# A residual block on one Trainium2 core: buffers of the first weight blocks, place of the forget logits' transposes, a transpose by DMA, and the engine of the last sums

## The chip, the cores and the metric

The kernel runs on one core of a Trainium2 chip. The metric is the device time of one execution in microseconds (us). A core has five instruction streams that run side by side and meet only through semaphores: TensorE (PE, its weight loads are listed as PEld), VectorE (DVE), ScalarE (ACT), GpSimd (POOL), and SyncE (SP), which here only issues DMAs.

## The reference

One layer of a hybrid encoder block; x is 256 tokens x 1024, all in fp32.

```python
h = rmsnorm(x, ffn1_pre_g)
x = x + 0.5 * rmsnorm(swiglu(h, ffn1_w_in, ffn1_w_down), ffn1_post_g)      # 1024 -> 2 x 2816 -> 1024

h = rmsnorm(x, mix_pre_g)
q_a, f_a, i_a, g_a, q_b, k_b, v_b, f_b, gates = split(h @ w_in)             # f_b: 8 forget logits a token
o_a = rmsnorm(hgrn2(q_a, f_a, i_a), hg_norm_g) * silu(g_a)                  # gated linear recurrence, 8 heads
c   = cumsum(log_sigmoid(f_b + fox_f_bias), axis=tokens)                    # 8 x 256
s   = q_b . k_b / sqrt(128) + c[query] - c[key], causal                     # 8 heads
o_b = softmax(s) @ v_b
y   = sigmoid(gate_a) * (o_a @ w_branch_a) + sigmoid(gate_b) * (o_b @ w_branch_b)
x   = x + rmsnorm(y @ w_out, mix_post_g)

x = x + rmsnorm(cross_attention(rmsnorm(x, mem_pre_g), rmsnorm(mem, mem_kv_g)), mem_post_g)
h = rmsnorm(x, ffn2_pre_g)
x = x + 0.5 * rmsnorm(swiglu(h, ffn2_w_in, ffn2_w_down), ffn2_post_g)
```

## The kernel before, in words

**Weights.** All large weights (some 145 MB) are read once, in units of 128 x 1024 floats (512 KB). `load_split` (L120) loads a unit into a buffer of the ring `raw` (four buffers), ScalarE casts it to `hi` (L128), VectorE computes the remainder `lo` (L129), and each product is made of three: hi.hi, hi.lo, lo.hi. The `raw` buffer is free for another load when `lo` is done. `hi` and `lo` have eight buffers each. SyncE issues the loads in program order and waits, in its own queue, for the buffer that the next load needs.

**Head.** The first four units, which are chunk 0 of the first FFN's input weights, come in another form: eight `head` blocks of 128 x 776 floats, block kb holding the kb-th 128 rows of x transposed (256 columns), the same rows of the weights (512) and the gains (8). The eight tiles share the four buffers of `raw` (L462). For each block ScalarE casts the weights (L475) and, but for the first, the x part (L262), and VectorE computes both remainders (L263, L477). Behind the head stand four ordinary units (chunk 1), then x itself in token order (`xs`, two loads, L482), whose place in SyncE's queue is given by `X_AT` (not ahead of the load with that number), and the columns of gains and the bias (L484, L485).

**First FFN.** Its gain is folded into the x part, and the token's 1/rms (`rstd`) is applied when a product is evacuated. Chunks 0 and 1 are computed first (`act_first`, L371: per block of 128 rows six products of 128 x 512, two token halves times three), into four PSUM banks; only then `norm_1` gives rstd from `xs` by ScalarE's sums of squares (L234) and a chain of small VectorE operations (L214 to L230). The evacuations (`act_evac`, L356 and L361) follow, mixed with the splits of the units of chunk 2, which is computed in the same manner.

**Forget logits.** They are the last eight columns of a group of weights with g_a; `zf` (128 x 8, one tile for each half of the tokens, L709) holds them times rstd. `forget(m)` (L717) turns both to 8 x 128 on TensorE, put behind product m of the log of products (`after` makes the scheduler issue them not before that product; they need not stand together), and then makes the bias, log-sigmoid (ScalarE) and running sum (VectorE) into `cc` (8 x 256). POOL stores `cc` to DRAM as `cd` (L733). It is called with m + 30, where m is the number of the first product of k_b's first half.

**Attention scores.** POOL loads `cd` back as rows spread to all partitions: `cbc` (L781) and two `cbm` (L785), on which it puts the causal mask (L788). The same sums as columns, `ct` (128 x 16), come from two transposes of `cc` on TensorE and a copy by VectorE (L794, L795). `fox_scores` (L799) uses them: VectorE adds `ct` and subtracts `cbc` or `cbm` (L817, L819), ScalarE makes the exponentials (L822).

**Gates.** Four bias rows `brow` (L878) have two buffers, which the early keys `E` of the recurrence (L582) use before them.

**End.** `post_last` (L302) computes the last half of the tokens: squares, rstd, then `x + t * r`. Columns 0 to 511 and 768 to 1023 are done by VectorE and stored through SyncE's queue, columns 512 to 767 by ScalarE (scaling), POOL (sum) and a store from ScalarE's queue (L325 to L333). For the first half of the tokens, and for the other layers, `post` does it in two VectorE operations of 512 columns (L298).

Of the kernel before, what the change touches and what calls it, by code (L numbers as in the profile page):

```python
# [11 lines left out]
F32 = mybir.dt.float32  # L12
F32R = mybir.dt.float32r
I32 = mybir.dt.int32
AF = mybir.ActivationFunctionType
ALU = mybir.AluOpType
AX = mybir.AxisListType

P = 128
D = 1024  # L20
T = 256
KB = D // P
# [25 lines left out]

WARM = 8

X_AT = 10


_ORDER = [
# [15 lines left out]
def block_kernel(ctx: ExitStack, tc: tile.TileContext, wts, head_in, gf_in, x_in, mem_in, memT_in, cols, rows, fbias, masks, out):  # L70
    nc = tc.nc
    V, S, G, PE = nc.vector, nc.scalar, nc.gpsimd, nc.tensor

    cp = ctx.enter_context(tc.tile_pool(name="consts", bufs=1))
    wp = ctx.enter_context(tc.tile_pool(name="weights", bufs=4))
    mp = ctx.enter_context(tc.tile_pool(name="data", bufs=21))
    sp = ctx.enter_context(tc.tile_pool(name="small", bufs=8))
# [5 lines left out]
    def MM(*args, **kw):  # L83
        log.append(PE.matmul(*args, **kw).ins)  # L84
# [9 lines left out]
    def nm(s):  # L94
        count[0] += 1
        return f"{s}_{count[0]}"

    def m4(shape, dt=F32, n="m"):
        return mp.tile(shape, dt, tag="m4", name=nm(n))

    def s1(n=1, dt=F32, name="s"):
        return sp.tile([P, n], dt, tag=f"s{n}", name=nm(name), bufs=16)
# [7 lines left out]
    def trp():  # L110
        return pp.tile([P, 512], F32, tag="tr", name=nm("tr"), bufs=2)
# [5 lines left out]
    def parts_of():  # L117
        return [wp.tile([P, D], F32R, tag=t, name=nm(t), bufs=8) for t in ("hi", "lo")]
# [31 lines left out]
    class Pair:  # L150


        def __init__(self, n=2):
            self.h, self.l = [], []
            for _ in range(n):
                self.more()
# [39 lines left out]
    ones = cp.tile([P, P], F32, name="ones")  # L196
    V.memset(ones, 1.0)
    ident = cp.tile([P, P], F32, name="ident")
    make_identity(nc, ident)

    warm = s1(name="warm")
# [31 lines left out]
    def ssq(dst, src):  # L233
        S.activation(junk[:, : src.shape[-1]], src, AF.Square, accum_out=dst)  # L234
# [67 lines left out]
    def post_last(ps, h, grow, factor):  # L302

        s = s1(2, name="ss2")
        ts = []
        for j in range(2):
            ssq(s[:, j : j + 1], ps[j])
            if j == 0:
                sums = s1(name="v")
                V.tensor_scalar(out=sums, in0=s[:, 0:1], scalar1=D * EPS, scalar2=None, op0=ALU.add)  # L310
            else:
                y = s1(name="y")
                S.activation(y, s[:, 1:2], AF.Sqrt, bias=sums)
                v = s1(name="v")
                V.tensor_tensor(out=v, in0=s[:, 1:2], in1=sums, op=ALU.add)
            t = sp.tile([P, 512], F32, tag="z2", name=nm("post"), bufs=3)
            V.scalar_tensor_tensor(out=t, in0=ps[j], scalar=-factor * 16.0, in1=grow[:, j * 512 : (j + 1) * 512], op0=ALU.mult, op1=ALU.mult)
            ts.append(t)
        z = s1(name="y")
        V.reciprocal(z, y)  # L320
        t = s1(name="t")
        V.scalar_tensor_tensor(out=t, in0=v, scalar=z, in1=z, op0=ALU.mult, op1=ALU.mult)
        r = s1(name="y")
        V.scalar_tensor_tensor(out=r, in0=t, scalar=3.0, in1=z, op0=ALU.subtract, op1=ALU.mult)
        for eng, a, b, queue in ((G, 512, 768, nc.scalar), (V, 0, 512, nc.sync), (V, 768, 1024, nc.sync)):  # L325
            xh = xs[:, h, a:b]
            t = ts[a // 512][:, a % 512 : a % 512 + b - a]
            if eng is G:
                S.activation(t, t, AF.Copy, scale=r)
                G.tensor_tensor(out=xh, in0=t, in1=xh, op=ALU.add)  # L330
            else:
                V.scalar_tensor_tensor(out=xh, in0=t, scalar=r, in1=xh, op0=ALU.mult, op1=ALU.add)
            queue.dma_start(out[h * P : (h + 1) * P, a:b], xh)  # L333


    def ffn(w_in, w_dn, X, r2, n_tok, i_row, first_half, second_half=None):
# [122 lines left out]


    X1 = Pair()
    heads = [wp.tile([P, D], F32, tag="raw", name=nm("head"), bufs=4) for _ in range(KB)]  # L462
    for kb in range(KB):
        loads.append(nc.sync.dma_start(heads[kb][:, : T + 512 + KB], head_in[kb]).ins)

    S.activation(warm, ones[:, 0:1], AF.Silu)
    wps = trp()
    for _ in range(WARM):
        MM(wps[:, :P], ones, ones, start=True, stop=True)
    for kb in range(KB):  # L470
        if kb % 2 == 0:
            cache[_AT["f1_in"] + kb // 2] = parts_of()
        hi, lo = (p[:, kb % 2 * 512 : kb % 2 * 512 + 512] for p in cache[_AT["f1_in"] + kb // 2])
        w = heads[kb][:, T : T + 512]
        S.copy(hi, w)  # L475
        gain_split(X1, kb, heads[kb][:, :T], heads[kb][:, T + 512 + kb : T + 512 + kb + 1], first=kb == 0)
        V.tensor_tensor(out=lo, in0=w, in1=hi.bitcast(F32), op=ALU.subtract)  # L477

    def norm_1():
        with tc.issue_after(loads[X_AT]):  # L480
            for h in range(2):
# [20 lines left out]
    for h in range(2):  # L502
        m = len(log)
# [70 lines left out]
    class Rec:  # L574


        def __init__(self, g):
            self.g, self.f = g, fT[g]
            self.aux = m4([P, D], n="aux")

            self.ATd = self.aux[:, 256:512]
            self.E = sp.tile([P, 512], F32, tag="brow", name=nm("early"), bufs=2)  # L582
            self.T = [self.aux[:, 512:], sp.tile([P, T], F32, tag="tq", name=nm("tq"), bufs=2)]
            G.memset(self.ATd, 0.0)
            self.AT = self.f
            self.cur = self.f.rearrange("p b h t -> p (b h t)")
            self.li = 0
# [126 lines left out]
    cc = sp.tile([8, T], F32, tag="fz", name="cc", bufs=1)  # L714
    cd = dp.tile([8, T], F32, name="cd")

    def forget(m):  # L717
        pf = trp()
        with after(m):
            for h in range(2):  # L720
                PE.transpose(pf[0:8, h * P : (h + 1) * P], zf[h], ident)
        V.tensor_scalar(out=fz, in0=pf[0:8, :T], scalar1=fb_s, scalar2=None, op0=ALU.add)
        V.scalar_tensor_tensor(out=fa, in0=fz, scalar=-1.0, in1=fz, op0=ALU.mult, op1=ALU.max)
        with tc.issue_after(sig_last):
            S.activation(fa, fa, AF.Exp, scale=-1.0)
        S.activation(fa, fa, AF.Ln, bias=1.0)
        V.scalar_tensor_tensor(out=fa, in0=fz, scalar=0.0, in1=fa, op0=ALU.min, op1=ALU.subtract)
        for h in range(2):
            cv, fv = (t[:, h * P : (h + 1) * P] for t in (cc, fa))
            if h:  # L730
                cv, fv = cv[:, ::-1], fv[:, ::-1]
            V.tensor_tensor_scan(out=cv, data0=ones[0:8, 0:1].to_broadcast([8, P]), data1=fv, initial=cc[:, P - 1 : P] if h else 0.0, op0=ALU.mult, op1=ALU.add)
        G.dma_start(cd, cc)  # L733
# [3 lines left out]
    for c in range(2):  # L737
        for name, lst, sc in (("k_b", kb_, 1.0), ("q_b", qb_, 1.0 / math.sqrt(128.0))):
            u = chunk(name, c)
            t = m4([P, 4, T], n=name)  # L740
            m = len(log)
            for j in range(2):
                ps = proj_col2(X2, u, (2 * j, 2 * j + 1))
                for i in range(2):
                    V.scalar_tensor_tensor(out=t[:, 2 * j + i], in0=ps[:, i], scalar=sc, in1=row2, op0=ALU.mult, op1=ALU.mult)
            lst.append(t)
            if c == 0 and name == "k_b":
                forget(m + 30)


    for li, m in enumerate(LEVELS + (64, 128)):
# [14 lines left out]
    for h in range(2):  # L766
# [8 lines left out]
        r = rstd_x(ps)  # L775
        for j in range(2):
            V.scalar_tensor_tensor(out=Gt[h][:, j * 512 : (j + 1) * 512], in0=ps[j], scalar=r, in1=Gt[h][:, j * 512 : (j + 1) * 512], op0=ALU.mult, op1=ALU.mult)


    cbc = m4([P, 8, P], n="cbc")  # L780
    G.dma_start(cbc, cd[:, 0:P].partition_broadcast(P))  # L781
    cbm = []
    for g in range(2):
        t = m4([P, 4, T], n="cbm")
# [2 lines left out]
            tv = t[:, :, b * P : (b + 1) * P]  # L787
            G.affine_select(out=tv, in_=tv, pattern=[[0, 4], [-sign, P]], compare_op=ALU.is_ge, fill=BIG, base=0, channel_multiplier=sign)  # L788
        cbm.append(t)

    ct = s1(16, name="ct")
    pc = trp()
    for h in range(2):
        PE.transpose(pc[:, h * 8 : h * 8 + 8], cc[:, h * P : (h + 1) * P], ident[0:8, 0:8])  # L794
    V.tensor_copy(ct, pc[:, :16])  # L795

    ps_, pT0s, pT1s = {}, [], []

# [61 lines left out]
    for c in range(2):  # L860
        u = chunk("v_b", c)
        t = m4([P, 2, 512], n="v_b")
# [12 lines left out]
    def gates(c):  # L875
        u = chunk("gates", c)
        z = m4([P, 2, 512], n="zg")
        brow = sp.tile([P, 512], F32, tag="brow", name=nm("brow"), bufs=2)  # L878
        with tc.issue_after(loads[-1]):
            nc.sync.dma_start(brow, rows[4 + c // 2, c % 2 * 512 : c % 2 * 512 + 512].partition_broadcast(P))  # L880
        for h in range(2):
            ps = mm()
            proj_tok(ps, X2, u, h)
            V.scalar_tensor_tensor(out=z[:, h], in0=ps, scalar=r2[h], in1=brow, op0=ALU.mult, op1=ALU.add)
        zs.append(z)

    m = len(log)
# [20 lines left out]
    for c in range(1, 4):  # L908
        gates(c)
# [14 lines left out]
    for c in range(2):  # L924
        for name, X, zc in (("br_a", OA, c), ("br_b", OB, 2 + c)):
            u = chunk(name, c)
            for h in range(2):
                z = zs[zc][:, h]
                m = len(log)
# [23 lines left out]
    m = len(log)  # L953
# [7 lines left out]
    m = len(log)  # L961
# [5 lines left out]
    m = len(log)  # L967
    for c in range(2):
        u = chunk("mk", c)
        KM.more()  # L970
        for j in range(2):
            js = slice(2 * j, 2 * j + 2)
            ps = proj_col2(M, u, (2 * j, 2 * j + 1))
            t = sp.tile([P, 2, T], F32, tag="z2", name=nm("km"), bufs=3)
# [25 lines left out]
    for h in range(2):  # L1000
        a, b = h * P, (h + 1) * P
# [3 lines left out]
        for i in range(4):  # L1005
            for j in range(2):
                kb = 2 * i + j
# [7 lines left out]
        p = m4([P, 4, T], n="pm")  # L1015
# [27 lines left out]
    m = len(log)  # L1043
# [15 lines left out]
    m = len(log)  # L1059
# [100 lines left out]
```

## Time and profile before

| | |
|---|---|
| median of 3 runs | 797.56 us (797.14 to 797.66) |
| the profiled execution, its own time | 798.41 us |
| its span in the trace | 796.6 us, granted TensorE clock 0.999 |
| ScalarE busy | 426.6 us (54%), x650 |
| VectorE busy | 519.8 us (65%), x824 |
| POOL busy | 11.7 us (1%), x29 |
| read from HBM | 145.67 MB, 184 GB/s over the span |
| head loads | 8, 388 KB each, median 3.8 us to landing |
| weight loads | 248, 512 KB each, median 4.4 us to landing |

Each row of a timeline gives the start, the duration, the engine, the line of the kernel, the operation with output and input, their size, and how many equal ones were merged; in brackets stands how long the engine had been idle and who ended that. An engine name with a q (SPq) is the engine's queue of issues. Rows of groups give minimum, median and maximum duration in ns, and the first and last start. Rows of stretches give the busy time and count on PE, PEld, DVE, ACT and POOL, then the granted clock, the busy share of the 16 DMA engines and GB/s. The rest of an execution's own time, 1.8 us here, lies outside the span.

### The profile page before, as it was taken

The numbers are of one execution on the slowest core, as the hardware profiler recorded it, in microseconds if no ns is written. First come the engines' busy times: TensorE is split into PE (matmuls) and PEld (weight loads), VectorE is DVE, ScalarE is ACT, GpSimd is POOL, SyncE is SP. The second block draws the span as 40 slices with busy tenths as digits, with TensorE's granted clock in tenths as the row PEclk, the third lists the DMA queues.
The fourth block names the chain that finished last, engine by engine and source line by source line (L and its number), as shares of the span: only waits on it lengthen the run. The fifth ranks groups of instructions, "written<-read, shape, count | busy, mean of one in ns | idle before, by whom it ended". The sixth has DMA issues, their size and how long they took to land.

```text
span 796.6 us, 12213 instructions
## 1 busy us (share of the span) xinstructions
PE 787.1 (99%) x4748; PEld 679.3 (85%) x4748; DVE 519.8 (65%) x824; ACT 426.6 (54%) x650; POOL 11.7 (1%) x29
## 2 busy tenths in 40 slices
PE   9999999999999999999999999999999999999996
PEld 7788888887899999998888888999888888888885
DVE  5774544557756997688675665965649754545543
ACT  5774434546754567458574345655647644434541
POOL 0000000000000100300000000000000000000000
PEclk9999999999999999999999999999999999999999
DMA  8886655565455454844486655456443656654521
GB/s 268 289 269 210 227 206 163 172 203 179 161 184 143 128 184 159 290 148 147 151 271 238 207 171 169 157 186 202 149 135 132 215 190 225 198 200 161 186 80 53
DMA packets 43689, 147.52 MB, mean 185 GB/s; under 512 B 4840, under 2 KB 8176, under 8 KB 43632
## 3 DMA queue, kind: packets, MB, share of 16 engines
q1 hardware_dynamic: 43024, 145.03, 54.9%
q0 software_dynamic: 464, 1.58, 0.6%
q8 instruction: 37, 0.61, 0.3%
q14 instruction: 20, 0.16, 0.1%
q10 hardware_dynamic: 144, 0.13, 0.0%
HBM read 145.67 MB, written 1.06 MB: 184 GB/s over the span
## 4 chain that ended last, share of the span: by engine, by line
PE 94%; DMA 3%; DVE 2%; ACT 1%; issue 0%; SPq 0%; DVEq 0%; ACTq 0%
PE mm L84 66%; PE acc L84 24%; PE tr L351 1%; DMA head<-in_head_dram 1%; PE tr L84 1%; DMA xs<-in_x_dram 1%; PE tr L271 1%; DMA raw<-in_wts_dram 1%; PE tr L834 0%; PE tr L920 0%; PE tr L1023 0%; ACT junk L234 0%; DVE lo L477 0%; DVE lT L263 0%; ACT hi L475 0%
## 5 line engine op out<-in xcount | busy, mean ns | idle before, releaser
L129 DVE TENSOR_TENSOR lo<-raw,hi 128x1024 fp32r<-128x1024 f32 (+1 forms) x260 | 311.4, 1206 | 127.7 <-ACT hi L128 118.8
L128 ACT CAST hi<-raw 128x1024 fp32r<-128x1024 f32 (+1 forms) x260 | 267.3, 1038 | 155.7 <-PE mm L84 81.9
L84 PE MATMUL mm<-lo,hT 128*128 128x512 f32 (+1 forms) x592 | 227.2, 386 | 0.7 <-DVE lo L129 0.7
L84 PE MATMUL mm<-hi,hT 128*128 128x512 f32 (+1 forms) x592 | 227.1, 386 | 0.1
L84 PE MATMUL mm<-hi,lT 128*128 128x512 f32 (+1 forms) x592 | 226.1, 385 | 0.0
L84 PEld LDWEIGHTS mm<-hi,hT 128*128 128x128 f32 x592 | 111.1, 188 | 22.4 <-ACT hT L262 0.6
L84 PEld LDWEIGHTS mm<-hi,lT 128*128 128x128 f32 x592 | 111.1, 188 | 21.7 <-DVE lT L263 0.5
L84 PEld LDWEIGHTS mm<-lo,hT 128*128 128x128 f32 x592 | 111.0, 188 | 21.5 <-DVE lo L129 1.1
L84 PE MATMUL acc<-hi,act 128*128 128x512 f32 x352 | 111.9, 390 | 0.0
L84 PE MATMUL mm<-hT,hi 128*128 128x256 f32 x384 | 109.1, 284 | 0.0
L84 PE MATMUL mm<-hT,lo 128*128 128x256 f32 x384 | 109.0, 284 | 0.0
L84 PE MATMUL mm<-lT,hi 128*128 128x256 f32 x384 | 108.9, 284 | 0.0
L84 PEld LDWEIGHTS acc<-hi,act 128*128 128x128 f32 x352 | 66.1, 188 | 13.1
L84 PEld LDWEIGHTS mm<-hT,hi 128*128 128x128 f32 x384 | 73.6, 192 | 0.4 <-PE mm L84 0.3
L84 PEld LDWEIGHTS mm<-hT,lo 128*128 128x128 f32 x384 | 73.6, 192 | 0.1
L84 PEld LDWEIGHTS mm<-lT,hi 128*128 128x128 f32 x384 | 73.6, 192 | 0.1
L84 PE MATMUL acc<-lo,act 128*128 128x512 f32 x176 | 70.0, 398 | 0.0
L356 ACT ACTIVATE sg<-mm,rstd 128x256 f32<-128x256 f32 x40 | 19.0, 475 | 74.8 <-PE mm L84 74.8
L361 DVE SCALAR_TENSOR_TENSOR at<-mm,rstd,sg 128x256 f32<-128x256 f32 x40 | 19.2, 480 | 56.6 <-ACT sg L356 56.6
L84 PEld LDWEIGHTS acc<-lo,act 128*128 128x128 f32 x176 | 33.1, 188 | 6.2
L84 PE MATMUL acc<-hi,hT 128*128 128x512 f32 x96 | 35.8, 401 | 0.1
L84 PE MATMUL acc<-hi,lT 128*128 128x512 f32 x96 | 35.2, 394 | 0.0
(195 smaller groups left out, 648.4 us busy)
## 6 DMA issues: line engine op xcount, KB each, us to landing
raw<-in_wts_dram SPq DMA_DIRECT2D x248, 512.0 KB, 4.4
raw<-in_gf_dram SPq DMA_DIRECT2D x12, 344.0 KB, 3.8
head<-in_head_dram SPq DMA_DIRECT2D x8, 388.0 KB, 3.8
grow<-in_rows_dram SPq DMA_DIRECT2D x4, 512.0 KB, 6.0
xs<-in_x_dram SPq DMA_DIRECT2D x2, 512.0 KB, 7.7
cbm<-cd POOLq DMA_DIRECT2D x2, 512.0 KB, 8.6
brow<-in_rows_dram SPq DMA_DIRECT2D x4, 256.0 KB, 5.0
memT<-in_memT_dram SPq DMA_DIRECT2D x2, 512.0 KB, 6.2
```

The source lines that it names most:

```text
L84: log.append(PE.matmul(*args, **kw).ins)
L128: S.copy(h, r)
L129: V.tensor_tensor(out=l, in0=r, in1=h.bitcast(F32), op=ALU.subtract)
L271: PE.transpose(ps[:, j * P : (j + 1) * P], src(kb), ident)
L351: PE.transpose(trv[:, j, h * P : (h + 1) * P], ats[c, h][:, j * P : (j + 1) * P], ident)
L356: silu = S.activation(sg, ps[:, :FC], AF.Silu, scale=r2[h])
L361: V.scalar_tensor_tensor(out=a, in0=ps[:, FC:], scalar=r2[h], in1=sg, op0=ALU.mult, op1=ALU.mult)
```

## The change

- The eight head blocks get eight buffers: four of `raw`, four of a new ring `extra`. The ring `brow` is gone; the early keys `E` and the four `brow` rows take buffers of `extra` (four) in its place. To make room, the scratch of POOL's DMA descriptors is set to 4096 bytes.
- `X_AT` goes from 10 to 11. In the head, the cast of a block is put behind the VectorE remainder of the block before.
- `forget` is called with m + 46 in place of m + 30.
- `ct` is loaded by two DMAs from `cd`, issued by POOL ahead of `cbc`, in place of two transposes and a copy.
- `post_last` does the last sums in two VectorE operations of 512 columns, both stored through SyncE's queue.

```diff
-X_AT = 10
+X_AT = 11
...
-        for eng, a, b, queue in ((G, 512, 768, nc.scalar), (V, 0, 512, nc.sync), (V, 768, 1024, nc.sync)):
+        for a, b in ((0, 512), (512, 1024)):
             xh = xs[:, h, a:b]
-            t = ts[a // 512][:, a % 512 : a % 512 + b - a]
-            if eng is G:
-                S.activation(t, t, AF.Copy, scale=r)
-                G.tensor_tensor(out=xh, in0=t, in1=xh, op=ALU.add)
-            else:
-                V.scalar_tensor_tensor(out=xh, in0=t, scalar=r, in1=xh, op0=ALU.mult, op1=ALU.add)
-            queue.dma_start(out[h * P : (h + 1) * P, a:b], xh)
+            V.scalar_tensor_tensor(out=xh, in0=ts[a // 512], scalar=r, in1=xh, op0=ALU.mult, op1=ALU.add)
+            nc.sync.dma_start(out[h * P : (h + 1) * P, a:b], xh)
...
-    heads = [wp.tile([P, D], F32, tag="raw", name=nm("head"), bufs=4) for _ in range(KB)]
+    heads = [wp.tile([P, D], F32, tag="raw" if kb < 4 else "extra", name=nm("head"), bufs=4) for kb in range(KB)]
...
-    S.activation(warm, ones[:, 0:1], AF.Silu)
+    warm_last = S.activation(warm, ones[:, 0:1], AF.Silu).ins
...
+    lo_last = warm_last
     for kb in range(KB):
...
-        S.copy(hi, w)
+        with tc.issue_after(lo_last):
+            S.copy(hi, w)
...
-        V.tensor_tensor(out=lo, in0=w, in1=hi.bitcast(F32), op=ALU.subtract)
+        lo_last = V.tensor_tensor(out=lo, in0=w, in1=hi.bitcast(F32), op=ALU.subtract).ins
...
-            self.E = sp.tile([P, 512], F32, tag="brow", name=nm("early"), bufs=2)
+            self.E = wp.tile([P, D], F32, tag="extra", name=nm("early"), bufs=4)[:, :512]
...
-                forget(m + 30)
+                forget(m + 46)
...
+    ct = s1(16, name="ct")
+    for h in range(2):
+        G.dma_start(ct[:, 8 * h : 8 * h + 8], cd[:, h * P : (h + 1) * P].rearrange("e p -> p e"))
     cbc = m4([P, 8, P], n="cbc")
...
-    ct = s1(16, name="ct")
-    pc = trp()
-    for h in range(2):
-        PE.transpose(pc[:, h * 8 : h * 8 + 8], cc[:, h * P : (h + 1) * P], ident[0:8, 0:8])
-    V.tensor_copy(ct, pc[:, :16])
...
-        brow = sp.tile([P, 512], F32, tag="brow", name=nm("brow"), bufs=2)
+        brow = wp.tile([P, D], F32, tag="extra", name=nm("brow"), bufs=4)[:, :512]
...
-    nc = _bacc.Bacc("TRN2", target_bir_lowering=False, num_devices=1)
+    nc = _bacc.Bacc("TRN2", target_bir_lowering=False, num_devices=1, dynamic_dma_scratch_size=4096)
```

## The prediction

> **What bounds the kernel now.** I read the profile's page first, then the list of waits for TensorE, then the timeline of the first 31 us, of the stretch around the forget logits, of the attention scores and of the end.
>
> ```profile
> span 796.6 us, 12213 instructions
> PE 787.1 (99%) x4748; PEld 679.3 (85%) x4748; DVE 519.8 (65%) x824; ACT 426.6 (54%) x650; POOL 11.7 (1%) x29
> ```
> ```profile
> PE mm L84 <- DVE lo L129: 0.7, 1, 0.7
> PE tr L721 <- DVE zf L709: 0.5, 1, 0.5
> ```
>
> TensorE is busy 99% of the span, and once it works it is kept waiting in few places: the first 31 us, one wait on zf, and the tail behind the last product. Everything else runs under the products. So an edit is worth what it takes out of TensorE's stream, out of those stalls, or out of the tail; the other engines count only where they keep TensorE waiting.
>
> **The head.** Three views of it follow (start, duration, engine, line, operation; in brackets the idle time before and who ended it): SyncE's queue, TensorE's weight loads, ScalarE.
>
> ```profile
> 0.75 9.32 SPq L464 DMA_DIRECT2D head<-in_head_dram  x8
> 11.00 5.03 SPq L127 DMA_DIRECT2D raw<-in_wts_dram  x4
> 16.09 0.90 SPq L482 DMA_DIRECT2D xs<-in_x_dram  x2
> ```
> ```profile
> 4.73 0.50 PEld L84 LDWEIGHTS acc<-hi,hT 128*128 128x128 f32 x2 [0.18 <-ACT hi L475]
> ...
> 9.59 0.42 PEld L84 LDWEIGHTS acc<-hi,hT 128*128 128x128 f32 x2
> ...
> 12.32 0.41 PEld L84 LDWEIGHTS acc<-hi,hT 128*128 128x128 f32 x2
> ...
> 14.03 0.30 PEld L84 LDWEIGHTS acc<-hi,hT 128*128 128x128 f32 x2 [0.39 <-ACT hT L262]
> ...
> 28.21 0.30 PEld L84 LDWEIGHTS mm<-hi,hT 128*128 128x128 f32 x2 [0.46 <-ACT hi L128]
> ...
> 30.10 0.30 PEld L84 LDWEIGHTS mm<-lo,hT 128*128 128x128 f32 x2 [1.12 <-DVE lo L129]
> ```
> ```profile
> 4.06 0.62 ACT L475 CAST hi<-head 128x512 fp32r<-128x512 f32 x1 [1.82 <-DMA head<-in_head_dram]
> ...
> 12.94 0.62 ACT L475 CAST hi<-head 128x512 fp32r<-128x512 f32 x1 [1.39 <-DMA head<-in_head_dram]
> ...
> 23.46 0.63 ACT L234 ACTIVATE junk<-xs 128x512 f32<-128x512 f32 x1 [0.20 <-DMA xs<-in_x_dram]
> ```
> ```profile
> 28.82 1.23 DVE L129 TENSOR_TENSOR lo<-raw,hi 128x1024 fp32r<-128x1024 f32 x1
> ```
>
> One block of the head is six products. From 9.59 to 12.32 two blocks pass undisturbed: 1.365 us a block, 0.2275 us a product. Chunks 0 and 1 are 96 products, 21.84 us; from 4.73 they would end at 26.57, but chunk 2 begins at 28.21: 1.64 us lost. Chunk 2's fifth product could load at 28.21 + 4 x 0.2275 = 29.12 and loads at 30.10: another 0.98. Of these 2.62 us, 9.59 - 4.73 - 3 x 1.365 = 0.77 fall in the first three blocks. That leaves 0.87 between block 3 and chunk 2 (0.35 of it where block 6 starts, 14.03 against 12.32 + 1.365 = 13.68), and the 0.98 behind it.
>
> What causes these later 1.85? SyncE spends 9.32 us on the eight head loads, because each of the last four waits until VectorE has done with an early block and its buffer is free; ScalarE then sits 1.39 us before block 6's cast. The four weight loads behind them begin at 11.00, and x, queued after these, at 16.09. x lands at 23.46. Only then come its squares, the rstd, the first evacuation and, behind that in the queues of ScalarE and VectorE, the splits of chunk 2's first unit, whose lo starts at 28.82 and ends when TensorE's wait does, 30.10.
>
> With eight buffers SyncE issues the eight loads without a wait. Now the weight loads wait for blocks 0 to 3, as the last four head loads did before; the last of those was issued by 0.75 + 9.32 = 10.07, so x leaves near 11, not 16.09. From there the DMA engines set the pace. Two stretches (the last column is GB/s):
>
> ```profile
> 5.00:10.00 5.00, 5.00 (x19) 3.64 (x20) 3.83 (x8) 3.80 (x8) 0.00 (x0) 1.00 0.85 266
> ```
> ```profile
> 22.00:28.00 6.00, 6.00 (x28) 4.78 (x26) 4.22 (x17) 5.19 (x11) 0.00 (x0) 1.00 1.01 396
> ```
>
> While buffers gate the loads it is 266; with many loads queued, 396. At 396 a head block (128 x 776 floats, 0.397 MB) takes 1.00 us, less than TensorE's 1.365, so the blocks run ahead of it. After block 0 (used from 4.06) come seven blocks, four weight loads of 0.524 MB and x of 1.05: 5.9 MB, 15 us, so x is there near 19 to 20, about four earlier. The rstd and the first splits move with it: lo of chunk 2's first unit ends near 26, where TensorE, not waiting from block 3 on, asks for it at 4.73 + 0.77 + 100 x 0.2275 = 28.25. What is late next is chunk 2's third unit, whose cast stands behind the evacuation of chunk 1: an evacuation, a cast and a lo, some 3 us after chunk 1 ends, and first wanted 24 products = 5.5 us after it. So the later 1.85 go entirely. The 0.77 of the first three blocks is mostly the splitting itself and stays; a deeper queue could take some of it. Value 1.9, bounds 0 (first rival) and 2.6.
>
> X_AT = 11 changes nothing: in the built order x stands behind the same four weight loads. The order that the edit forces on ScalarE (issue_after(lo_last)) is the order it had.
>
> **Forget logits.**
>
> ```profile
> 296.12 0.28 PE L84 MATMUL mm<-hT,lo 128*128 128x256 f32 x1
> 296.86 0.27 PE L721 MATMUL tr<-ident,zf 128*8 128x128 f32 x1 [0.46 <-DVE zf L709]
> ```
> ```profile
> 296.58 0.22 DVE L709 TENSOR_SCALAR zf<-mm,rstd 128x8 f32<-128x8 f32 x1
> ```
> ```profile
> 298.55 0.46 DVE L722 TENSOR_SCALAR fz<-tr,fb_s 8x256 f32<-8x256 f32 x1
> ```
>
> A product of this shape takes half the columns of the head's, 0.12 us, so the second transpose was due at 296.24 and started at 296.86: 0.62 lost. In the built order the first transpose goes 16 products later and the second only 5, both together: 5 x 0.12 = 0.6 later. The second is due at 296.85, and zf is ready at 296.80. Stall left: 0 to 0.1; value 0.55, bounds 0.3 and 0.62. Behind the wait VectorE's fz starts at 298.55, in the order of its own queue, over 1 us after the transposes will be done (near 297.1); nothing gets later.
>
> **Sums as columns by DMA.**
>
> ```profile
> 318.63 0.94 POOL L781 DMA_DIRECT2D cbc<-cd  x1 [3.42 <-DVE q L647]
> ```
> ```profile
> cbc<-cd POOLq DMA_DIRECT2D x1, 512.0 KB, 6.1
> ```
> ```profile
> 330.63 3.02 POOL L788 TENSOR_SCALAR_AFFINE_SELECT cbm<-cbm 128x512 f32<-128x512 f32 x2 [1.28 <-DMA cbm<-cd]
> ```
> ```profile
> 348.25 0.20 PEld L794 LDWEIGHTS tr<-ident,cc 8*128 8x128 f32 x2
> ```
> ```profile
> 350.12 0.34 DVE L819 SCALAR_TENSOR_TENSOR p<-tr,ct,cbm 128x128 f32<-128x128 f32 x1
> ```
> ```profile
> 361.42 0.67 ACT L866 ACTIVATE v_b<-mm,rstd 128x512 f32<-128x512 f32 x1
> ```
>
> Two transposes leave TensorE: 0.20 us. The small copy leaves VectorE at a place where TensorE doesn't wait for it: nothing. Added are two POOL loads of 1024 single floats each, ahead of cbc and both cbm in POOL's queue. The nearest row is cbc, which holds POOL 0.94 us. It has 8 x 128 = 1024 separate pieces as well, so by pieces the two make 1.9 us; if POOL's time goes by cbc's 128 partitions, 1024 elements cost eight times as much, 15.0 us for both. The masks on POOL end at 333.65 and their first reader starts at 350.12: 16.5 us of cover, and the edit costs nothing while POOL's extra is below that. I take 1.9, as the pieces are equal in number. The smaller scratch for POOL's descriptors could make POOL wait until earlier loads have drained (cbc lands 6.1 us after its issue), under the same cover. Value 0.2, bounds 0.2 and the third rival.
>
> [...]
>
> **Last sums.**
>
> ```profile
> L332 DVE SCALAR_TENSOR_TENSOR xs<-post,y,xs x2: 753/850/947, 791.7 to 792.3; 128x512 f32<-128x512 f32 x1, 128x256 f32<-128x256 f32 x1
> L298 DVE SCALAR_TENSOR_TENSOR xs<-post,y,xs x14: 745/748/753, 188.4 to 785.0; 128x512 f32<-128x512 f32 x14
> L333 SPq DMA_DIRECT2D out_dram<-xs x2: 332/332/333, 792.4 to 793.3; - x2
> L300 SPq DMA_DIRECT2D out_dram<-xs x2: 344/348/351, 785.1 to 785.8; - x2
> ```
>
> Beside POOL's sum VectorE's 256 columns took 947 ns, longer than 512 columns elsewhere (748). Now VectorE does two halves of 512. The pair at L300 is that very shape: its stores leave 0.7 us apart (785.1, 785.8), against 0.9 us (792.4, 793.3). So the last store leaves 0.2 us earlier; that it is twice as large may take some of it back. Value 0.2, bounds 0 and 0.3. ScalarE's own store, earlier than the last one, was not on the path.
>
> **Other moves.** The gates' bias rows stand up to four loads earlier in SyncE's queue and lose their buffer waits, and the early keys move to the new buffers; TensorE waits for no weights in that stretch, so nothing.
>
> **Sum.** 1.9 + 0.55 + 0.2 + 0.2 = 2.85. The profiled execution took 798.41 us (span 796.6 and 1.8 around it), the median of the runs 797.56, 0.85 less; the saving is the same for both: 795.6 for a profiled one, 794.7 for the median.
>
> **The rivals.** A difference under 0.2% (1.6 us) I take as none, about what a measurement of this kernel can tell.
>
> First, the head gains nothing: the DMA rate, not the buffers, bounds the early stream, x still lands near 23 and lo of chunk 2 is ready near 30; TensorE comes to it sooner and waits longer. For it: the engines are 85% busy even at 266 GB/s. Against: 396 once loads are queued. Then 0.55 + 0.2 + 0.2 = 0.95 remain: 796.6.
>
> Second, on the slower side: the DMA engines serve all eight queued blocks side by side instead of in turn. Then block 0 lands with the others, 7 x 1.00 us after 4.06, and TensorE starts 7.0 us later, though without stalls. Less 2.6 and 0.95, that is 3.45 slower: 801.0. It decides as soon as block 0 lands over 3.55 us late. Against it: four blocks are queued together now, and the first is in use at 4.06.
>
> Third, the column loads are late: POOL pays by the element (15.0 us for both), and the engines take as long over 1024 floats as over cbc's 1024 pieces (6.1 us each, 12.2). The masks, queued behind, end 27.2 later, 10.7 beyond the cover. The scores wait, and on ScalarE the evacuation of v_b (361.42) stands behind them; once its two PSUM banks are full TensorE loses nearly all of the 10.7. Less 2.85: 805.4. It decides from 16.5 us on. Against it: the row by pieces. [...]
>
> **How the numbers follow.** The forecast has 0.79, the first rival 0.13, the second 0.05, the third 0.03. Predicted 794.7. The forecast's own span runs from 793.8 (2.6 + 0.62 + 0.2 + 0.3 = 3.7) to 795.9 (head gain 0.8); the range takes in the first rival: 793.6 to 797.0, which leaves out the slower cases. Faster by over 0.2%: 0.79; within: 0.13; slower: 0.08.
>
> **What would show it.** In the changed profile: the eight head loads issued in about 4 us with no wait behind them; x landing before 21; no TensorE wait between 10 and 32 us, chunk 2 starting near 27.3 (4.73 + 0.77 + 21.84); no wait on zf, or one under 0.1; two ct loads on POOL near 318 and the masks done before 345; the last store leaving 0.7 us after the one before it. I am wrong if TensorE still waits for chunk 2's lo, if block 0's cast starts after 4.5, or if VectorE waits for ct.

## Result, and the profile after

The changed kernel takes 796.18 us (median of 17 runs, 795.45 to 796.67) where the kernel before, on the same chip, takes 797.96 (17 runs, 796.84 to 798.83): ratio 0.9978, 95% interval 0.9971 to 0.9986. That is 1.78 us or 0.22% faster, just more than the 0.2% taken as no difference. Forecast were 794.7 and a range of 793.6 to 797.0: the direction is right, the median is inside the range, and the saving is 1.1 smaller than the forecast 2.85. The profiled execution took 796.3.

The page's first lines, and TensorE's list of waits (us in total, times, longest):

```profile
span 794.5 us, 12205 instructions
...
PE 785.5 (99%) x4746; PEld 679.1 (85%) x4746; DVE 519.4 (65%) x823; ACT 425.8 (54%) x649; POOL 11.2 (1%) x30
```
```profile
PE tr L84 <- DVE ones L197: 1.1, 1, 1.1
PE acc L84 <- ACT hT L262: 0.7, 1, 0.7
```

The waits on lo (0.7) and on zf (0.5) are gone from this list; a wait on hT, in the first blocks, is new.

The head, as before: SyncE's queue, then TensorE's weight loads, then ScalarE, then VectorE.

```profile
0.75 4.44 SPq L459 DMA_DIRECT2D head<-in_head_dram  x8
5.31 5.24 SPq L127 DMA_DIRECT2D raw<-in_wts_dram  x4
10.60 0.90 SPq L479 DMA_DIRECT2D xs<-in_x_dram  x2
```
```profile
4.43 0.55 PEld L84 LDWEIGHTS acc<-hi,hT 128*128 128x128 f32 x2
...
8.51 0.30 PEld L84 LDWEIGHTS acc<-hi,hT 128*128 128x128 f32 x2 [1.12 <-ACT hT L262]
...
10.03 0.42 PEld L84 LDWEIGHTS acc<-hi,hT 128*128 128x128 f32 x2
...
27.73 0.41 PEld L84 LDWEIGHTS mm<-hi,hT 128*128 128x128 f32 x2
...
28.63 0.41 PEld L84 LDWEIGHTS mm<-lo,hT 128*128 128x128 f32 x2
```
```profile
7.43 0.62 ACT L472 CAST hi<-head 128x512 fp32r<-128x512 f32 x1 [1.57 <-DMA head<-in_head_dram]
...
18.73 0.63 ACT L234 ACTIVATE junk<-xs 128x512 f32<-128x512 f32 x1 [0.22 <-DMA xs<-in_x_dram]
```
```profile
24.09 1.22 DVE L129 TENSOR_TENSOR lo<-raw,hi 128x1024 fp32r<-128x1024 f32 x1
```

SyncE issues the eight loads in 4.44 us instead of 9.32, x leaves at 10.60 and is in use at 18.73, 4.7 us earlier, and lo of chunk 2's first unit starts at 24.09 in place of 28.82. From block 3 (10.03) to chunk 2 (27.73) TensorE takes 17.70 us for 78 products of 0.2275 = 17.75: nothing is lost, and chunk 2's fifth product loads at 28.63, where it was 30.10. What has grown is the loss in the first three blocks: 10.03 - 4.43 - 3 x 1.365 = 1.50 (0.77 before), since block 2's cast begins only at 7.43.

The forget logits and the scores (TensorE's weight loads, VectorE, POOL):

```profile
295.48 0.08 PEld L718 LDWEIGHTS tr<-ident,zf 128*8 128x8 f32 x1 [0.16 <-DVE zf L706]
```
```profile
347.57 1.59 PEld L84 LDWEIGHTS acc<-k_b,q_b 128*128 128x128 f32 x8 [0.31 <-DVE G L774]
```
```profile
346.77 1.41 DVE L774 SCALAR_TENSOR_TENSOR G<-acc,rstd,G 128x512 f32<-128x512 f32 x2
...
348.21 0.34 DVE L813 SCALAR_TENSOR_TENSOR p<-tr,ct,cbm 128x128 f32<-128x128 f32 x1
```
```profile
316.78 1.82 POOL L779 DMA_DIRECT2D ct<-cd  x2 [3.06 <-DMA cd<-cc]
318.59 0.88 POOL L781 DMA_DIRECT2D cbc<-cd  x1
...
332.04 1.51 POOL L788 TENSOR_SCALAR_AFFINE_SELECT cbm<-cbm 128x512 f32<-128x512 f32 x2 [1.26 <-DMA cbm<-cd]
```

The second transpose of zf waits 0.16. The two column loads hold POOL 1.82 us, and the masks end at 333.55, 14.7 before their first reader. But the scores' weights now wait 0.31 for VectorE's G, which nothing in the trace of before did.

The end (groups: minimum, median, maximum in ns, first and last start):

```profile
L327 DVE SCALAR_TENSOR_TENSOR xs<-post,y,xs x2: 747/750/752, 789.7 to 790.4; 128x512 f32<-128x512 f32 x2
```
```profile
L328 SPq DMA_DIRECT2D out_dram<-xs x2: 333/333/333, 790.5 to 791.2; - x2
```

The second store leaves 0.7 after the first, as forecast.

### The profile page after: what moved, and what is told of

It is laid out like the page before. It is cut to its first block, busy times and chain, and to the rows that moved or that the text cites. A ratio compares the mean times of both kernels' runs of the same rounds, so it can differ in the third digit from the quotient of the medians.

```text
span 794.5 us, 12205 instructions
## 1 busy us (share of the span) xinstructions
PE 785.5 (99%) x4746; PEld 679.1 (85%) x4746; DVE 519.4 (65%) x823; ACT 425.8 (54%) x649; POOL 11.2 (1%) x30
## 3 DMA queue, kind: packets, MB, share of 16 engines
HBM read 145.68 MB, written 1.06 MB: 185 GB/s over the span
## 4 chain that ended last, share of the span: by engine, by line
PE 97%; DVE 1%; DMA 1%; issue 0%; ACT 0%; SPq 0%; DVEq 0%; ACTq 0%
PE mm L84 67%; PE acc L84 26%; PE tr L346 1%; PE tr L271 1%; PE tr L84 1%; DMA head<-in_head_dram 1%; PE tr L828 0%; DVE lo L129 0%; PE tr L914 0%; PE tr L1017 0%; ACT hi L128 0%; SPq L459 0%; DVE G L774 0%; DVE xs L327 0%; DVE q_b L742 0%
```

## Experiments

Eleven kernels ran. e1 to e4 make one part of the change each, on the kernel before; e11 edits e3; the others edit the changed kernel. Each kernel's own profile is compared at the same places.

### One part at a time

e1 has the head's part of the diff alone (buffers, `E` and `brow`, scratch, `X_AT`, the casts' order), e2 only `forget(m + 46)`, e3 only the column loads, e4 only the last sums.

> The kernel before with the head's edits alone (eight buffers, E and the bias rows in the new ring, POOL's scratch, x one unit later, casts in order). Theory: of the 2.1 us by which the two profiled spans differ, 1.4 are made here, so 796.2 against 797.6, and chunk 2 starts and goes on without a wait. Two readings of why the first three blocks lost more than before (1.50 us against 0.77): if the longer queue of loads delays block 2, its cast starts near 7.4 again and the gain stays at 1.4; if that was chance, the cast starts near 7.0 as before and the gain is 2.1.

> The kernel before with the forget logits' transposes 16 products later, and nothing else. Theory: the wait on zf (0.5 in the list of waits) goes and nothing takes its place: 0.6 faster, kept to the end. Rival: VectorE's fz, now later against the products, makes the cumulative sums and with them the scores late: then less than 0.3 is left behind the scores.

> The kernel before with the sums as columns by two POOL loads, and nothing else. Theory (give-back): the two transposes cost TensorE some 0.4 us at that place, and the second scores' weights then wait 0.3 for VectorE's G, which the transposes had covered: 0 to 0.1 faster in all. Rival (as forecast): 0.2 faster with no wait. Third: with the large scratch the masks end as late as with the small one (333.6); if POOL's own time per load falls below 0.9 us, the scratch had a price.

> The kernel before with the last sums all on VectorE, and nothing else. Theory: the stretch from the last product to the end of the span is 0.15 us shorter, no more, since the last store is twice as large. Rival: nothing, because the last store lands later by what it is issued earlier.

Measured against the kernel before, 797.62 (33 runs), with 11 runs each:

| kernel | median, us | ratio, 95% interval | saving by medians |
|---|---|---|---|
| e1, head | 796.54 | 0.9985, 0.9977 to 0.9994 | 1.08 |
| e2, forget | 797.36 | 0.9998, 0.9989 to 1.0007 | 0.26 |
| e3, ct | 797.40 | 0.9997, 0.9988 to 1.0006 | 0.22 |
| e4, last sums | 797.57 | 1.0001, 0.9992 to 1.0010 | 0.05 |

Only the head's saving stands clear of the interval. The medians of the parts add up to 1.61, the whole gave 1.78.

e1 gained less than either of its two readings expected, 1.4 or 2.1. The profiles show why: e2, e3 and e4 have the old head, unchanged, and its stalls differ from one profile to the next. Chunk 2's fifth product, weight loads of e2, e3 and e4 in turn:

```profile
29.42 0.30 PEld L84 LDWEIGHTS mm<-lo,hT 128*128 128x128 f32 x2 [0.19 <-DVE lo L129]
```
```profile
29.23 0.30 PEld L84 LDWEIGHTS mm<-lo,hT 128*128 128x128 f32 x2 [0.75 <-DVE lo L129]
```
```profile
29.05 0.30 PEld L84 LDWEIGHTS mm<-lo,hT 128*128 128x128 f32 x2 [0.23 <-DVE lo L129]
```

With four buffers that product loads at 30.10 (before), 29.42, 29.23, 29.05, and at 29.80 in a later kernel (e11): mean 29.52, spread 1.05. With eight buffers and one queue: 28.63 (after), 28.36 (e1), 28.36 (e5), 28.32 (e6), 28.61 (e8): mean 28.46, spread 0.31. The means are 1.06 apart, e1's 1.08. The profile that the prediction was worked from was the worst of five.

Block 2's cast begins at 6.99, 7.20, 6.68, 7.04 and 6.81 with four buffers and at 7.43, 7.12, 7.14, 7.12 and 7.41 with eight. So part of the 0.44 by which the profile after was later than the one before was chance. A mean difference of 0.3 remains, which speaks for the first reading of e1, that the longer queue delays block 2, but does not settle it: e1's 7.12 lies within the spread of the old head.

The wait on zf varies in the same way where the transposes stand in their old place. Their weight loads in e1, e3 and e4:

```profile
295.26 0.08 PEld L723 LDWEIGHTS tr<-ident,zf 128*8 128x8 f32 x1 [0.64 <-DVE zf L711]
```
```profile
295.41 0.08 PEld L721 LDWEIGHTS tr<-ident,zf 128*8 128x8 f32 x1
```
```profile
295.49 0.08 PEld L716 LDWEIGHTS tr<-ident,zf 128*8 128x8 f32 x1 [0.32 <-DVE zf L704]
```

0.64, none, 0.32, and 0.66 in e11. In e2, with the later place, both transposes run together without a wait:

```profile
296.01 0.18 PEld L721 LDWEIGHTS tr<-ident,zf 128*8 128x8 f32 x2
```

The lead is kept to the end (e2's last product starts 1.19 before that of the kernel before, and the products behind the scores 1.24); the rival, late sums behind fz, doesn't show. So the theory for e2 holds as to the mechanism, but with the stall that the old place has on average, about 0.45, rather than 0.6.

e3's second scores show the give-back again, in a kernel with the large scratch and the old head:

```profile
346.60 1.20 PEld L84 LDWEIGHTS tr<-k_b,q_b 128*128 128x128 f32 x10
348.11 1.59 PEld L84 LDWEIGHTS acc<-k_b,q_b 128*128 128x128 f32 x8 [0.31 <-DVE G L777]
```

The same two rows in the kernel before:

```profile
348.46 1.19 PEld L84 LDWEIGHTS tr<-k_b,q_b 128*128 128x128 f32 x10
...
349.57 1.60 PEld L84 LDWEIGHTS acc<-k_b,q_b 128*128 128x128 f32 x8
```

There they are 1.11 apart, here 1.51. What the missing transposes save ahead of the first row, 0.4, the wait for G takes back before the second: net nothing, as the give-back theory said. POOL's two column loads take 0.90 and 0.94 here, 0.89 and 0.94 with the small scratch: for two loads it has no price in POOL's time. The masks end at 331.4 here, 2.2 earlier than with the small scratch; one profile of each doesn't show whether the scratch has a part in that.

e4: from the start of the last product to the end of the span it is 7.35 us (787.75 to 795.1), against 7.46 before (789.14 to 796.6) and 7.31 after (787.19 to 794.5). The other profiles agree: 7.45 to 7.53 with the old last sums (e1, e2, e3), 7.29 to 7.38 with the new ones (e5, e6, e7, e9, e12). So 0.11 to 0.15, the theory's size; the medians can't show it.

### Who gave the transposes' gain back

```diff
-    def load_split(src, n=512):
+    def load_split(src, n=512, behind=None):
...
-        V.tensor_tensor(out=l, in0=r, in1=h.bitcast(F32), op=ALU.subtract)
+        with tc.issue_after(behind) if behind else nullcontext():
+            V.tensor_tensor(out=l, in0=r, in1=h.bitcast(F32), op=ALU.subtract)
...
+            last = V.scalar_tensor_tensor(...).ins      # G
+        if h == 0:
+            hold[_AT["v_b"] + 7] = last                 # that unit's lo goes behind G
```

> The changed kernel, with one VectorE remainder (the last unit of v_b's weights, 1.2 us, standing inside the rstd chain of the recurrence's output) put behind G. If the gain of the two removed transposes was given back because G comes too late, G now starts 1.2 us earlier, the 0.31 wait of the scores' weights goes, and the saving against before rises from 2.00 to 2.40 at that place: 0.3 to 0.4 faster than the changed kernel. Rival: the wait is for something else that ends with G (the squares on ScalarE), and then it stays, at 0.2 to 0.3.

Its VectorE and TensorE rows:

```profile
345.50 1.41 DVE L776 SCALAR_TENSOR_TENSOR G<-acc,rstd,G 128x512 f32<-128x512 f32 x2
```
```profile
346.69 1.60 PEld L84 LDWEIGHTS acc<-k_b,q_b 128*128 128x128 f32 x8
```

G starts 1.27 earlier than in the changed kernel, and the wait is gone: it was G, and G was late because a remainder stood in the middle of its rstd chain. Against the changed kernel this profile is 0.27 ahead when it comes to the scores (345.80 against 346.07, as much as it was behind the head), 0.65 at the products behind them and 0.57 at the last product, so 0.30 to 0.38 were gained here, as expected. The time is 795.95 us (ratio to before 0.9975, 0.9966 to 0.9984). The times don't show the gain: e6, below, in effect repeats the changed kernel, and it took 796.01 on the same chip.

### Why block 2 lands late

e6 put the issue of blocks 4 to 7 behind ScalarE's cast of block 0:

```diff
+        if kb == 0:
+            with tc.issue_after(hi_last):
+                for k in range(4, KB):
+                    load_head(k)
```

> The changed kernel, with the loads of head blocks 4 to 7 issued only behind ScalarE's cast of block 0 (near 4.3) in place of at once. If a queue of eight delays block 2, it lands near 6.9 as with four buffers (6.66 to 7.18 in four profiles) and the first three blocks lose about 0.8. If the length of the queue has no part in it, block 2 lands between 7.1 and 7.4 or anywhere in the spread of the others, and the time is that of the changed kernel, within 0.3.

```profile
0.75 4.86 SPq L459 DMA_DIRECT2D head<-in_head_dram  x8
```

This failed as an experiment: the edit orders the scheduler's list, but SyncE does not wait for ScalarE, and the eight loads still leave within 4.86 us, the first six at the old times. It is a repeat of the changed kernel: 796.01 us (0.9977, 0.9968 to 0.9987), block 2's cast at 7.12. Whether a shorter queue brings block 2 forward by the remaining 0.3 is open.

e7 issues two of the eight loads from ScalarE:

```diff
+        queue = nc.scalar if kb in (1, 3) else nc.sync
```

> The changed kernel, with the loads of head blocks 1 and 3 issued by ScalarE in place of SyncE (block 1 near 0.8, block 2 then near 1.2 instead of 1.7 on SyncE). In all six profiles so far block 2 lands 1.9 to 2.6 us behind block 1, where 1.0 is the time of a block at full rate. If SyncE's queue makes that gap, block 2 lands below 6.3 and the kernel is about 1 us faster. If it is made in the DMA engines or the memory at that time (4 to 6 us), block 2 lands near 7 and nothing changes; block 0 and 1 served side by side would land later, and TensorE would start late by up to 1.

ScalarE, and stretches of the trace (the last columns are the clock, the DMA engines' busy share and GB/s):

```profile
5.07 1.14 ACT L475 CAST hi<-head 128x512 fp32r<-128x512 f32 x2 [2.38 <-DMA head<-in_head_dram]
```
```profile
4.00:6.00 2.00, 1.11 (x5) 0.82 (x5) 0.90 (x3) 0.93 (x2) 0.00 (x0) 1.00 1.02 405
```

The same stretch of the changed kernel:

```profile
4.00:6.00 2.00, 2.00 (x9) 1.76 (x9) 1.62 (x4) 1.30 (x3) 0.00 (x0) 1.00 0.86 227
```

The outcome is the second expectation's: block 2 is cast at 7.05, and blocks 0 and 1 were served side by side (block 0's cast at 5.07 instead of 3.65, the weights of the first product 1.31 late), which is the second rival of the prediction at work between two queues. Its reason is refuted, though: the rate between 4 and 6 us does not fall, it is 405 GB/s, where the changed kernel has 227 and the other kernels with one queue have 242 to 349. The slower start and the faster stretch cancel in this profile: chunk 2's fifth product loads at 28.36, as in e1 and e5. The time is 796.01 us (0.9986, 0.9977 to 0.9995), but six of the eleven runs took 795.71 to 796.01 and five 797.43 to 798.10. The profile is of one of the six; what the five lost is not shown.

e9 and e12, on top of e5, give ScalarE only one load, block 2 in e9 and block 1 in e12, issued near 1.05 so that block 0 has the engines to itself:

```diff
+    heads_act = (2,)            # e12: (1,)
     for kb in range(KB):
-        loads.append(nc.sync.dma_start(...).ins)
+        if kb not in heads_act:
+            loads.append(nc.sync.dma_start(...).ins)
...
+    for kb in heads_act:
+        with tc.issue_after(warm_last):
+            warm_last = nc.scalar.dma_start(...).ins
```

In e12 each block's cast and x part are put behind the cast of the block before, so that the order on all three engines is that of e5.

> The changed kernel with the edit of e5 (the VectorE remainder behind G) and with the load of head block 2 alone issued by ScalarE, behind its warm-up near 2.3; the others stay in SyncE's queue. In e7, with loads in two queues from the start, the rate no longer falls between 4 and 6 us (391 to 450 GB/s, against 155 to 300 in every kernel with one queue), but blocks 0 and 1 were served side by side and TensorE began 1.3 late. If a second queue fills the gap of the first, block 2 now lands below 6.5 with blocks 0 and 1 as early as before, the first three blocks lose about 0.7 less and the kernel is 0.7 to 1 faster than the changed one. Rival: block 2, issued 0.6 later, is served behind or beside block 3, lands near 7 again, and only e5's 0.2 is left.

```profile
3.74 0.62 ACT L479 CAST hi<-head 128x512 fp32r<-128x512 f32 x1 [1.50 <-DMA head<-in_head_dram]
5.79 0.62 ACT L479 CAST hi<-head 128x512 fp32r<-128x512 f32 x1 [1.43 <-DMA head<-in_head_dram]
...
6.72 0.60 ACT L479 CAST hi<-head 128x512 fp32r<-128x512 f32 x1
```

Block 0 is as early as ever (3.74), and when block 1's cast can begin, at 5.79, block 2 is there already: its cast follows without a wait. The rate from 4 to 6 us is 383 GB/s (over the same stretch the kernels with one queue have 227 to 349, more than the 300 of the expectation). But the load that came early was the wrong one, and TensorE waits for block 1: 795.79 us (0.9975, 0.9966 to 0.9984). Chunk 2's fifth product loads at 28.33, 0.30 before the changed kernel's but only 0.03 before that of e5: the head gained nothing, and what is left is e5's share, as the rival had it.

> The changed kernel with the edit of e5 and with the load of head block 1, not 2, issued by ScalarE near 1.05; the order of all work on ScalarE, VectorE and TensorE is that of e5. In e9 the three first loads of the two queues landed at 3.72, 4.66 and 5.76 and the rate stayed at 376 to 391 GB/s, but the second to land was block 2, and TensorE, which needs block 1 next, waited for it. If that is all, block 1 now lands near 4.7 and block 2 near 5.8, TensorE starts near 4.45 and the first three blocks lose under 0.5 in place of 1.50 in the changed kernel: 1 to 1.4 faster than the changed kernel, near 795.0. Rival: what limits the first blocks is the split on ScalarE and VectorE, some 2 us from a landing to the products; then two thirds of the 1.50 stay and the time is that of e9.

```profile
3.87 0.62 ACT L479 CAST hi<-head 128x512 fp32r<-128x512 f32 x1 [1.62 <-DMA head<-in_head_dram]
4.78 0.62 ACT L479 CAST hi<-head 128x512 fp32r<-128x512 f32 x1 [0.29 <-DMA head<-in_head_dram]
...
6.20 0.62 ACT L479 CAST hi<-head 128x512 fp32r<-128x512 f32 x1 [0.40 <-DMA head<-in_head_dram]
```
```profile
4.54 0.50 PEld L84 LDWEIGHTS acc<-hi,hT 128*128 128x128 f32 x2
...
9.18 0.41 PEld L84 LDWEIGHTS acc<-hi,hT 128*128 128x128 f32 x2
```
```profile
27.77 0.41 PEld L84 LDWEIGHTS mm<-lo,hT 128*128 128x128 f32 x2
```

Block 2 is cast at 6.20, no product of the head waits, and the first three blocks lose 9.18 - 4.54 - 3 x 1.365 = 0.55 where they lost 1.50 in the changed kernel and 1.19 to 1.49 in e1, e5, e6 and e8, whose eight loads stand in one queue too. Chunk 2's fifth product loads at 27.77, 0.86 before the changed kernel's 28.63; but that one is the latest of the five, and before their mean, 28.46, it is 0.69. Against e5, which differs from it only in the head, 0.59 is gained there and 0.39 is left at the last product. This is the fastest version: 795.35 us (6 runs, 794.74 to 795.79) against 797.65 (10 runs), ratio 0.9968, 0.9956 to 0.9981. The expected 1 to 1.4 over the changed kernel is not reached in full, and the intervals of the two ratios overlap: that e12 is the faster of the two rests on the traces.

### What the column loads can cost

e8 adds 22 more column loads ahead of `cbc` to the changed kernel, e11 the same to e3, whose scratch for POOL's descriptors has its full size:

```diff
+    extra = cp.tile([P, 16 * 11], F32, name="extra")
+    for k in range(22):
+        G.dma_start(extra[:, 8 * k : 8 * k + 8], cd[:, k % 2 * P : k % 2 * P + P].rearrange("e p -> p e"))
     cbc = m4([P, 8, P], n="cbc")
```

> The changed kernel, with 22 more column loads of the same form on POOL between ct and cbc; what they load is not used. They take 22 x 0.91 = 20.0 us of POOL. In the changed kernel the masks end at 333.55 and are first read at 348.21, a cover of 14.7, so the masks now end 5.3 too late. By the third rival's mechanism the scores wait and TensorE loses nearly all of that: 4 to 5.3 slower than the changed kernel. Rival: the v_b products and the filled banks hide it, and less than 1 is lost. If a load's price rises when many are queued (scratch full), the loss is larger by that.

The group on POOL, its idle time, and VectorE's first reader of a mask:

```profile
L782 POOL DMA_DIRECT2D extra<-cd x22: 882/882/892, 317.8 to 357.7; - x22
its engine sat idle before it (us, times) until:
  issue: 21.3, 14
```
```profile
365.97 0.35 DVE L816 SCALAR_TENSOR_TENSOR p<-tr,ct,cbm 128x128 f32<-128x128 f32 x1 [17.66 <-POOL cbm L791]
```

816.92 us against 797.95, ratio 1.0238 (1.0224 to 1.0252): 19.0 slower than the kernel before and 20.7 slower than the changed one, where 4 to 5.3 were expected. The price by pieces held (882 ns a load), but POOL paused 21.3 us between the loads, and the masks end 34.2 later instead of 20. Beyond the cover the loss is one for one, as the third rival had it: 34.2 less 14.7 is 19.5, VectorE waits 17.7, TensorE stands 18.1 and then runs at half its rate for a while (its weight loads 0.43 us apart in place of 0.23, below).

> The kernel before with the column loads (as e3) and the same 22 more of them, with POOL's descriptor scratch left at its full size instead of 4096 bytes; what the 22 load is not used. In e8 POOL paused 21.3 us between them, 1.9 us from load to load, and the kernel was 20.7 slower. If the small scratch made the pauses, the loads now follow each other every 0.88, the masks end near 353 and the loss is near 5. If the engines can take no more such loads than one in 1.9 us, the loss stays near 20.

```profile
L785 POOL DMA_DIRECT2D extra<-cd x22: 880/882/890, 319.9 to 341.5; - x22
...
  DMA extra<-cd: 2.9, 5
  issue: 0.3, 1
```
```profile
343.40 1.04 ACT L128 CAST hi<-raw 128x1024 fp32r<-128x1024 f32 x1 [4.15 <-DMA raw<-in_wts_dram]
```
```profile
318.00:345.00 27.00, 27.00 (x230) 27.00 (x229) 14.06 (x19) 9.19 (x10) 23.05 (x27) 1.00 0.93 180
```

805.34 us (4 runs, 803.89 to 810.62) against 798.01, ratio 1.0110 (1.0081 to 1.0139). With the full scratch the pauses fall from 21.3 us to 3.2, of which 2.9 end with the landing of an earlier load: the small scratch made most of them. But the kernel is still 7.3 slower than the one before. The profile, which is of the slowest of the four runs (810.62), shows a way that neither theory had: the loads, no longer held back, keep the DMA engines 93% busy at 180 GB/s (with two column loads, in the changed kernel, the same stretch has 79% at 262), the weights land late (ScalarE waits 4.15 for one cast), ScalarE's squares and with them G are late, and TensorE waits 10.4 for G. This hides the expected way and doesn't refute it: the masks end at 358.1, 8.0 after their first reader started in the kernel before (350.12), so they would have been late too. What the other three runs lost by is not shown.

## Why the prediction was right or wrong

**Direction: right; range: right by its width.** The head's later stalls and the zf stall were the gain, and 796.18 lies within 793.6 to 797.0. But it lies above the forecast's own span, 793.8 to 795.9; the range reaches so far only because it takes in the first rival (796.6), whose mechanism did not come. Part of that is the kernel before, which took 797.96 in the 17 runs where the forecast started from 797.56 in three. The saving, 1.78, lies just inside the forecast's own span, which goes from 3.7 down to 1.75 (0.8 + 0.55 + 0.2 + 0.2; that gives 795.8, not the 795.9 written). The second and third rival did not come either.

**The head's mechanism: right; its size: mis-sized, 1.9 against 1.06.** Everything behind block 3 went as written: loads issued in 4.4 us, x leaving near 11 and there at 18.7, nothing lost between block 3 and chunk 2, no wait for lo. Two terms were off. First, the sum was made against the stalls of one execution, and they were the largest of five: 0.6 of the 2.62 belonged to that execution, not to the kernel. Second, the step "the 0.77 of the first three blocks is mostly the splitting itself and stays" failed. It did not stay: the changed kernel loses 1.50, because block 2 lands late, and the deeper queue took none of it away. Nor was it mostly the splitting: in the profile before, 0.40 of the 0.77 passes in block 0, 0.21 ahead of block 2 and 0.16 in block 2, where TensorE waits for VectorE's remainder. With the same splitting and block 2 early, e12 loses 0.55, all but 0.02 of it in block 0. There TensorE doesn't wait, but its first two pairs of weight loads take 0.50 and 0.76, later pairs 0.41 to 0.42; in the profiles before and after single ones take up to 0.33 there, later ones 0.19. They take 0.33 each in e8 too, at a granted clock of 0.50, but here the clock is 1.00 (4 to 6 us, in all three profiles), so why they are slow stays open.

**"Chunk 2 starts near 27.3": 27.73.** TensorE started 0.30 earlier than assumed and lost 0.73 more.

**Forget logits: right in kind, 0.55 forecast.** The wait fell from 0.66 to 0.16 in the two first profiles, outside the forecast 0 to 0.1; over five profiles of the old place it was 0.66, 0.64, 0, 0.32 and 0.66, 0.46 on average, and over eight of the new one it was 0 or 0.16, so about 0.4 is what the edit is worth in the traces (by medians 0.26 in e2, within the interval).

**Columns by DMA: the price right, the gain wrong.** The loads took 0.91 each, forecast 0.94; the masks were 14.7 early. The 0.2 taken for the transposes failed: the prediction asked who is late when a stall goes, but not when work goes. TensorE came to the scores 0.4 sooner, and VectorE's G was next. e3 and e5 show it. The price went by pieces, as taken: 0.91 us a load beside cbc's 0.88, where the third rival had 15.0 for both. The guess that the small scratch could make POOL wait is borne out by e8 and e11 for 24 loads (pauses of 21.3 us with the small scratch, 3.2 with the full one), not for two.

**Last sums: right.** The store left 0.2 earlier, and 0.11 to 0.15 of it reached the end of the span.

## What to carry to other kernels

The stalls behind the head's loads and the one on zf differed from one profile to the next (by 1.05 and 0.66 us over five), in code that was the same there: before an edit is priced at the stall it removes, read that stall in several profiles, or take less than one shows. When work is taken off the busiest engine, look for the engine that this work had been covering (here VectorE, whose G then kept the scores' weights waiting 0.31), and move that one's chain in the same edit. A load that costs little in its issuer's queue can still cost the DMA engines (e11's took 0.88 us each on POOL, and the engines were 93% busy for 27 us); price it in both places.

## What the runs showed of the hardware

**A gap in a single queue.** In all ten profiles with the eight head blocks in SyncE's queue alone, block 2's cast begins 1.9 to 2.6 us behind block 1's, and the rate between 4 and 6 us is 227 to 296 GB/s with eight buffers, 290 to 349 with four. With one or two of the loads in ScalarE's queue the rate is 405 (e7), 383 (e9) and 338 (e12, no more than the kernel before has), and in e12 block 2's cast begins 1.4 behind block 1's. From 8 to 12 us, later in the stream, a second queue makes no difference: the changed kernel moves 415 GB/s with one and e7 416 with two. From 4 to 6 us it is otherwise: e7's 405 and e9's 383 are above all ten. That the second queue as such closes the gap is not shown: in e12 block 2's load was also issued 0.5 earlier (at 1.20 against 1.67), and no kernel issued it earlier in a single queue. Why one queue leaves a gap there was not settled.

**TensorE after a stall.** Behind e8's stall of 18.1 us TensorE's weight loads stand 0.43 us apart, and from 376 on 0.23; the granted clock (third column from the right) is 0.50 from 370.5 to 374.5, 0.88 from 375 to 379 and 1.00 from 380 to 390:

```profile
370.50:374.50 4.00, 4.00 (x10) 3.15 (x11) 4.00 (x11) 0.14 (x1) 0.00 (x0) 0.50 0.00 0
375.00:379.00 4.00, 4.00 (x17) 3.26 (x16) 3.74 (x11) 3.68 (x15) 0.00 (x0) 0.88 0.00 0
380.00:390.00 10.00, 10.00 (x50) 8.38 (x49) 7.33 (x8) 6.25 (x14) 0.00 (x0) 1.00 0.53 177
```

The half rate lasted from 370.4 to 376.1, 5.6 us, and added some 2.6 us to the stall. What set that length is not shown.
